# A decoder layer on one core: TensorE's instructions kept in the program's order, and norm sums, rows, cross scores and transposes at other places

## The chip, the core and the metric

The kernel runs on one core of a Trainium2 chip. The metric is the device time of one execution, in microseconds (us). Of the core's engines the text speaks of TensorE (PE, matmuls; PEld are its weight loads), VectorE (DVE), ScalarE (ACT), GpSimd (POOL) and SyncE (SP), whose queue issues most of the DMAs.

## The reference

One layer on x of 256 tokens by 1024, in fp32, with RMSNorm ahead of each part:

```
x = x + 1/2 * SwiGLU_1(RMSNorm(x))
h = RMSNorm(x); q, k, v = split(h @ w_in)     # 12 heads dilated attention, 4 heads block attention, head width 64
x = x + concat(RMSNorm(group A), RMSNorm(group B)) @ w_out
x = x + CrossAttn(RMSNorm(x), RMSNorm(mem))   # 4 heads of width 256, 256 memory tokens
x = x + 1/2 * SwiGLU_2(RMSNorm(x))
out = RMSNorm(x)
rms_norm(x, g) = x * rsqrt(mean(x * x) + 1e-6) * g
```

With 256 tokens there is one block, and the patterns together come down to causal attention with a table per head and distance (the bias, plus the log of how many patterns reach a distance).

## The kernel before

Activations lie transposed, features on the partitions and the 256 tokens in the free dimension. Each fp32 weight tile (128 x 1024, 512 KB) is loaded by SP's queue into one of 4 `raw` buffers and split into one of 8 `w` buffers: a high part (ACT, L122) and the rest, the low part (DVE, L123). Activations are split in the same way into slots (`split`, L310 and L311, or L313 and L314 where a gain is applied). A product is the sum of high x high, high x low and low x high: `mmT_run` does the first two in one 512 wide pass (L221, the slot holds high and low side by side) and the third in a 256 wide pass (L225); `mm3` (L185 to L187) does three passes, `mm2` (L202, L203) is used for the cross output. PSUM is a pool of 8 banks.

The stages in order, by the trace: start and first chunk of gate_up1 (0 to 36 us), gate_up1 (to 139), downT (to 201), `qkv` and `attend` for two head groups (to some 283), cross keys and values (to 340), w_out (to 363), `cross_qp` with the cross scores (to 397), `cross_o` and w_co (to 424), gate_up2 (to 550), the second down product and the tail.

A norm (`Stats`) is deferred: the products run on x times gain without the factor 1/rms, which is applied to their result. `add` sums squares (ACT L327, GpSimd L332). `_col` sums over the partitions with two matmuls by ones (L344), scales (`ms`, DVE L347), takes the power -1/2 on GpSimd (`col`, L349) and writes it on two diagonals (`dg`, L353). `_rows` spreads it over all partitions with two matmuls (L359) and copies the result to `R` (L361).

Where such side work stands is set by a clock in the program: each matmul helper calls `tick` with a duration, `later(delay, fn)` puts `fn` on a list, and `fn` is written out once the clock has passed. `done` (L335) places `_col` at `delay` and `_rows` at `delay + gap`; `scores` and `turn` of `cross_qp` are placed in the same way (L623 and L648), as are `bias_table` (L88, its matmul L95) and the eight gathers from its scratch table. `cross_qp`'s `scores(h)` takes 12 passes for two token blocks, a softmax on DVE and ACT (`cmx`, `cnm`, `cpt`, `crl`, L634 to L644); `turn(h)` transposes the result (L652).

What is so written is then ordered once more by the scheduler of the tile framework, engine by engine. Only `start()` stands under `tc.manual_schedule()` and keeps the written order:

```
    with tc.manual_schedule():
        pu0 = start()
    hid = gate_up(w_gu1, xs, st, (None, bias_table), (pg0, pu0))
```

In `qkv` each 256 wide block of q and k is put together from its two halves and scaled by R at once (`scaled`, L284). In `start` the gain row `grow` is loaded on ACT's queue behind the first quarter of x.

Of the kernel before, what the change touches and what calls it, by code (L numbers as in the profile page):

```python
# [16 lines left out]
P = 128  # L17
# [11 lines left out]
def layer_kernel(ctx, tc, x_in, mem_in, g_ffn1, w_gu1, w_dn1, g_mix, w_in, rel_bias, g_out_a, g_out_b,  # L29
# [13 lines left out]
    def bank():  # L43
        return psp.tile([P, 512], F32, tag="bank", name="bank")
# [43 lines left out]
    def bias_table():  # L88
# [4 lines left out]
        nc.sync.dma_start(rbt, rel_bias)  # L93
        ps = bank()
# [221 lines left out]
    class Stats:  # L316
# [18 lines left out]
        def done(self, rows=True, delay=7.0, gap=4.5):  # L335
            later(delay, self._col)
            if rows:
                later(delay + gap, self._rows)
            return self
# [118 lines left out]
    def qkv(g, xs, st):  # L458
        q, k, v = slot(F32), slot(F32), slot(F32)
        for j, base_a, base_b in ((0, 0, 2304), (1, 768, 2560), (2, 1536, 2816)):  # L460
            wk = colchunk(w_in, base_a, 512) if g == 0 else colchunk2(w_in, base_a + 512, base_b)
            if j == 2:
                for tb in range(2):
                    ps = bank()
                    proj(ps, wk, xs, tb)
                    nc.scalar.activation(v[:, tb * 512:tb * 512 + 512], ps, AF.Copy, scale=st.column(tb))
                continue
            for blk, ps in enumerate(projT(wk, xs, 4, spread=(g == 0 and j == 0))):
                dst = (q, k)[j][:, blk * 256:(blk + 1) * 256]
                scaled(dst, [ps], st.rows(), (0.125, 1.0)[j])  # L470
        return q, k, v
# [149 lines left out]
    def cross_qp(xs, K, st):  # L621
# [3 lines left out]
        def scores(h):  # L625
# [20 lines left out]
            later(3.8, turn, h)  # L646
# [12 lines left out]
        for c in range(2):  # L659
            for blk, ps in enumerate(projT(colchunk(w_cq, c * 512, 512), xs, 4, spread=(c == 0))):  # L660
# [7 lines left out]
                if blk % 2:  # L668
                    later(1.8 + (2.0 * (blk // 2) if c == 0 else 0.0), scores, c * 2 + blk // 2)
# [29 lines left out]
    def start():  # L699
        load_x(0, 256)  # L700
        nc.scalar.dma_start(grow[0:8], g_ffn1.rearrange("l (k p) -> (l k) p", p=P))
# [40 lines left out]
        for k in range(KT):  # L742
# [4 lines left out]
            if k == 5:  # L747
                up.extend(colchunk(w_gu1, FF, 512))
                keep(3)
                st.done(delay=7.5)  # L750
# [14 lines left out]
    hid = gate_up(w_gu1, xs, st, (None, bias_table), (pg0, pu0))  # L765
    xs, st, block = next_x("mix")
    downT(w_dn1, hid, block)
    st.done()

    OT = [slot(F32), slot(F32)]  # L770
    stA, stB = Stats(768), Stats(256)
    ot = []

    def head_pair(kt, op):
        st = stA if kt < 6 else stB
        st.add(op)
        if kt == 5:
            st.done(delay=5.0)
            later(11.0, lambda: out_split(OT, stA.rows(), range(3), ot))
        elif kt == 7:  # L780
            st.done(delay=5.0)
            later(11.0, lambda: out_split(OT, stB.rows(), range(3, 4), ot))

    mxs, mst = mem_side()
    qkv0 = qkv(0, xs, st)
    attend(0, *qkv0, OT, 7.0, head_pair)
    qkv1 = qkv(1, xs, st)
    attend(1, *qkv1, OT, 6.0, head_pair)
    K = cross_k(mxs, mst)
    cross_v(mxs, mst, 0)  # L790
    cross_v(mxs, mst, 1)
    until(lambda: len(ot) == 4)
    xs, st, block = next_x("cross")
    addT(w_out, ot, block)
    st.done(rows=False)
    PT = cross_qp(xs, K, st)
    OT = []
    cross_o(V, PT, OT, (0, 1))
    xs, st, block = next_x("ffn2")
    addT(w_co, OT, block, 4, lambda: cross_o(V, PT, OT, (2, 3)))  # L800
    st.done()

    xt = []

    def to_tokens():
        xt2 = const.tile([P, 2, D], F32, tag="big", name="xt", bufs=2)
        for tb in range(2):
            t = xt2[:, tb]
            for hf in range(2):
                ps = bank()  # L810
                for i in range(4):
                    nc.tensor.transpose(ps[:, i * P:(i + 1) * P], X[hf * 4 + i][:, tb * P:(tb + 1) * P], ident)
                nc.vector.tensor_copy(t[:, hf * 512:hf * 512 + 512], ps)
            xt.append(t)

    hid = gate_up(w_gu2, xs, st, (None, to_tokens))
    gfin = const.tile([P, D], F32, tag="big", name="gfin", bufs=2)
    nc.scalar.dma_start(gfin, g_final.unsqueeze(0).broadcast_to([P, D]))
    HALVES = ((0, 512), (512, 512))
    ps = [[bank() for _ in HALVES] for _ in range(2)]  # L820

    def step(k, tb, w, p, c0, n, first, last):
        h, l = act(hid, k)
        t = slice(tb * P, tb * P + P)
        mm3(p, h[:, t], l[:, t], w[:, 0, c0:c0 + n], w[:, 1, c0:c0 + n], k == first, k == last)

    TAIL = 4
    rest = []
    for k in range(FK):
        w = wload((lambda raw: raw, w_dn2[0, k * P:(k + 1) * P, :], 1024))  # L830
        if k < FK - TAIL:
            for tb in range(2):
                for i, (c0, n) in enumerate(HALVES):
                    step(k, tb, w, ps[tb][i], c0, n, 0, FK - TAIL - 1 if (tb, i) == (1, 1) else FK - 1)
        else:
            rest.append((k, w))

    def add_down(tb, p, c0, n):
        nc.vector.scalar_tensor_tensor(xt[tb][:, c0:c0 + n], p, 0.5, xt[tb][:, c0:c0 + n], OP.mult, OP.add)

    add_down(1, ps[1][1], 512, 512)
    late = [bank()[:, :256] for _ in range(2)]
    PIECES = (((0, 512, ps[0][0], 0), (512, 512, ps[0][1], 0)),
              ((0, 512, ps[1][0], 0), (512, 256, late[0], FK - TAIL), (768, 256, late[1], FK - TAIL)))
    for tb in range(2):
        ss = small.tile([P, 3], F32, tag="fss", name="fss")
        ms = small.tile([P, 3], F32, tag="fms", name="fms")
        junk = work.tile([P, 1024], BF, tag="u1", name="junk")
        xg = slot(F32)
        for i, (c0, n, p, first) in enumerate(PIECES[tb]):  # L850
            sl = slice(c0, c0 + n)
            for k, w in rest:
                step(k, tb, w, p, c0, n, first, FK - 1)
            add_down(tb, p, c0, n)
            nc.scalar.activation(junk[:, sl], xt[tb][:, sl], AF.Square, accum_out=ss[:, i:i + 1])
            nc.vector.tensor_scalar(ms[:, i:i + 1], ss[:, i:i + 1], 1.0 / D, ms[:, i - 1:i] if i else 1e-6,
                                    OP.mult, OP.add)
            nc.vector.tensor_tensor(xg[:, sl], xt[tb][:, sl], gfin[:, sl], OP.mult)
        r = small.tile([P, 1], F32, tag="fr", name="fr")
        nc.gpsimd.tensor_tensor(r, ms[:, len(PIECES[tb]) - 1:len(PIECES[tb])], mhalf[:, 0:1], OP.pow)  # L860
        o = out[0, tb * P:(tb + 1) * P]
        nc.vector.tensor_scalar(xg[:, 0:512], xg[:, 0:512], r, None, OP.mult)
        nc.sync.dma_start(o[:, 0:512], xg[:, 0:512])
        nc.scalar.activation(xg[:, 512:1024], xg[:, 512:1024], AF.Copy, scale=r)
        nc.scalar.dma_start(o[:, 512:1024], xg[:, 512:1024])
# [44 lines left out]
```

## Time and profile before

| | us |
|---|---|
| median of 3 runs | 618.31 |
| lowest, highest | 616.53, 618.38 |
| the profiled execution | 619.02 |
| its span, first to last instruction | 617.1 |
| TensorE busy in it | 601.6 (97%) |
| VectorE busy | 446.0 (72%) |
| ScalarE busy | 350.3 (57%) |
| GpSimd busy | 57.5 (9%) |
| mean granted TensorE clock | 0.997 |

Busy time is the time in which an engine has an instruction under way. A row of a timeline has the start in us, the duration of the run of like instructions in us, the engine, the line, the operation, what is written and read, and how many; a bracket at its end gives the idle time of the engine just before it and what ended that. Matmuls overlap, so the starts tell their pace better than their durations.

### The profile page before, as it was taken

The page shows a single profiled execution, that of the slowest core. Times are in us where ns is not written, and L with a number is a line of the kernel's source. Part 1 is how long each engine was busy: PE and PEld are TensorE (multiplying, and loading weights), DVE is VectorE, ACT ScalarE, POOL GpSimd, SP SyncE. Part 2 cuts the span into 40 slices and gives each one's busy share as a digit, 9 for nine tenths or more (in the row PEclk, how much of TensorE's full clock was granted, in tenths as well). Part 3 has the DMA queues.
Part 4 walks back from the last instruction along what each step waited for, and adds up shares of the span by engine and source line. Part 5 has one row for each costly group of instructions (what it writes and reads, how often), then busy time and mean ns, then how long its engine had stood idle before and what let it go on. Part 6 is the DMA issues. An engine that isn't in the chain of part 4 may idle for free.

```text
span 617.1 us, 9493 instructions
## 1 busy us (share of the span) xinstructions
PE 601.6 (97%) x3488; PEld 518.0 (84%) x3488; DVE 446.0 (72%) x764; ACT 350.3 (57%) x614; POOL 57.5 (9%) x90
## 2 busy tenths in 40 slices
PE   7999999999999899999999999999999999999995
PEld 7987888888899788877877888888888888888885
DVE  3888648898574767775888788868888788794424
ACT  5757426665463666554756566757564565664313
POOL 0000300000010231121311031003100000000000
PEclk9999999999999999999999999999999999999998
DMA  7776996677856637335344646334656646576501
GB/s 233 248 224 195 228 230 203 204 229 229 246 186 198 191 121 237 104 124 185 104 137 141 211 160 206 102 104 138 204 162 213 205 159 223 165 244 202 166 1 68
DMA packets 58989, 110.02 MB, mean 178 GB/s; under 512 B 3760, under 2 KB 14608, under 8 KB 58944
## 3 DMA queue, kind: packets, MB, share of 16 engines
q1 hardware_dynamic: 56848, 104.44, 53.9%
q0 software_dynamic: 832, 2.88, 2.7%
q10 hardware_dynamic: 1264, 2.10, 0.9%
q8 instruction: 27, 0.44, 0.3%
q14 instruction: 18, 0.15, 0.1%
HBM read 107.58 MB, written 1.84 MB: 177 GB/s over the span
## 4 chain that ended last, share of the span: by engine, by line
PE 84%; DVE 6%; ACT 3%; DMA 3%; issue 2%; POOL 1%; ACTq 0%; POOLq 0%
PE bank L221 39%; PE bank L225 20%; PE bank L186 6%; PE bank L185 6%; PE bank L187 6%; DVE w L123 3%; ACT w L122 2%; DMA raw<-in_w_ffn_gu_dram 1%; PE bank L235 1%; PE bank L484 1%; PE bank L531 1%; PE bank L515 1%; DMA raw<-in_w_co_dram 1%; DVE slot L314 1%; DMA grow<-in_g_ffn_dram 1%
## 5 line engine op out<-in xcount | busy, mean ns | idle before, releaser
L221 PE MATMUL bank<-slot,w 128*128 128x512 f32 x1162 | 364.6, 397 | 1.3 <-DVE g L282 0.8
L123 DVE TENSOR_TENSOR w<-raw,w 128x1024 fp32r<-128x1024 f32 (+1 forms) x197 | 239.0, 1227 | 72.9 <-ACT w L122 72.1
L122 ACT ACTIVATE w<-raw 128x1024 fp32r<-128x1024 f32 (+1 forms) x197 | 201.8, 1050 | 96.4 <-PE bank L187 41.2
L225 PEld LDWEIGHTS bank<-slot,w 128*128 128x128 f32 x1162 | 213.8, 188 | 49.1 <-issue 1.5
L225 PE MATMUL bank<-slot,w 128*128 128x256 f32 x1162 | 227.2, 280 | 0.0
L221 PEld LDWEIGHTS bank<-slot,w 128*128 128x128 f32 x1162 | 179.9, 189 | 6.3 <-issue 1.7
L267 ACT ACTIVATE hv<-bank 128x256 f32<-128x256 f32 x120 | 44.0, 376 | 32.6 <-PE bank L225 27.1
L185 PE MATMUL bank<-w,slot 128*128 128x512 f32 (+1 forms) x156 | 60.7, 389 | 0.0
L186 PE MATMUL bank<-w,slot 128*128 128x512 f32 (+1 forms) x156 | 60.1, 385 | 0.0
L187 PE MATMUL bank<-w,slot 128*128 128x512 f32 (+1 forms) x156 | 59.9, 384 | 0.0
L185 PEld LDWEIGHTS bank<-w,slot 128*128 128x128 f32 x156 | 29.3, 188 | 6.1 <-issue 0.5
L187 PEld LDWEIGHTS bank<-w,slot 128*128 128x128 f32 x156 | 29.3, 188 | 5.9
L310 ACT ACTIVATE slot<-u 128x512 fp32r<-128x512 f32 x22 | 13.9, 630 | 35.7 <-DVE u L405 35.7
L186 PEld LDWEIGHTS bank<-w,slot 128*128 128x128 f32 x156 | 29.4, 188 | 5.4
L332 POOL TENSOR_TENSOR ssq<-ssq,sq 128x256 f32<-128x256 f32 x28 | 24.2, 865 | 71.6 <-ACT sq L327 71.1
L268 DVE TENSOR_TENSOR u<-bank,hv 128x256 f32<-128x256 f32 x40 | 16.8, 421 | 10.8 <-ACT hv L267 10.7
L314 DVE SCALAR_TENSOR_TENSOR slot<-X,gT,slot 128x256 fp32r<-128x256 f32 x30 | 19.9, 673 | 6.4 <-ACT slot L313 6.3
L400 ACT ACTIVATE g<-g 128x512 f32<-128x512 f32 x22 | 13.8, 631 | 18.7 <-DVE g L282 18.7
L268 DVE TENSOR_TENSOR g<-bank,hv 128x256 f32<-128x256 f32 x40 | 16.4, 421 | 10.6 <-ACT hv L267 10.6
L502 ACT ACTIVATE pt<-pt,nm 128x128 f32<-128x128 f32 (+1 forms) x32 | 14.2, 445 | 15.1 <-DVE nm L500 15.1
L332 POOL TENSOR_TENSOR ssq<-sq 128x256 f32<-128x256 f32 x6 | 5.2, 870 | 182.1 <-ACT sq L327 182.1
L313 ACT ACTIVATE slot<-X,gT 128x256 fp32r<-128x256 f32 x30 | 14.9, 506 | 12.3 <-DVE X L293 12.3
(132 smaller groups left out, 523.4 us busy)
## 6 DMA issues: line engine op xcount, KB each, us to landing
raw<-in_w_ffn_gu_dram SPq DMA_DIRECT2D x88, 512.0 KB, 4.7
raw<-in_w_ffn_down_dram SPq DMA_DIRECT2D x44, 512.0 KB, 4.6
raw<-in_w_ckv_dram SPq DMA_DIRECT2D x16, 512.0 KB, 6.0
raw<-in_w_in_dram SPq DMA_DIRECT2D x12, 512.0 KB, 3.7
raw<-in_w_in_dram SPq DMA_DIRECT2D x24, 256.0 KB, 4.1
raw<-in_w_out_dram SPq DMA_DIRECT2D x8, 512.0 KB, 5.1
raw<-in_w_cq_dram SPq DMA_DIRECT2D x8, 512.0 KB, 6.0
raw<-in_w_co_dram SPq DMA_DIRECT2D x8, 512.0 KB, 4.0
```

The source lines that it names most:

```text
L122: nc.scalar.activation(w[:, 0, a:b], raw[:, a:b], AF.Copy)
L123: nc.vector.tensor_tensor(w[:, 1, a:b], raw[:, a:b], w[:, 0, a:b].bitcast(F32), OP.subtract)
L185: nc.tensor.matmul(ps, ah, bh, start=start, stop=False)
L186: nc.tensor.matmul(ps, al, bh, start=False, stop=False)
L187: nc.tensor.matmul(ps, ah, bl, start=False, stop=stop)
L221: nc.tensor.matmul(ps, w[:, 0, o + blk * P:o + (blk + 1) * P], both(xs, k), start=k == first, stop=False)
L225: nc.tensor.matmul(ps[:, :256], w[:, 1, o + blk * P:o + (blk + 1) * P], both(xs, k)[:, :256], start=False, stop=k == last)
L267: nc.scalar.activation(t, ps[:, 256:], AF.Copy)
L268: nc.vector.tensor_tensor(out, ps[:, :256], t, OP.add)
L313: nc.scalar.activation(h, src, AF.Copy, scale=g)
L314: nc.vector.scalar_tensor_tensor(l, src, g, h.bitcast(F32), OP.mult, OP.subtract)
L332: (eng or nc.gpsimd).tensor_tensor(new, self.ss, sq, OP.add)
```

## The change

Everything behind `start()` goes under `tc.manual_schedule(engines={PE})`: TensorE keeps the written order, the other engines are still ordered by the scheduler. The matmul of the bias table and what follows from it become `bias_rows`, placed 4.0 behind the loads. The default delay of a norm's sums goes from 7.0 to 9.5; the first norm's gap from 4.5 to 2.8; the delays of head group B from 5.0 and 11.0 to 8.0 and 14.0. `qkv` only puts the halves of q and k together, and scales q in one instruction and k in two once the key product is done. The cross scores of the first two heads go from 1.8 and 3.8 to 2.6 and 4.6, the transposes from 3.8 to 5.0. The gain row is issued ahead of x.

```diff
@@ bias_table
         nc.sync.dma_start(rbt, rel_bias)
+        later(4.0, bias_rows, lnt, oht)
+
+    def bias_rows(lnt, oht):
         ps = bank()
         nc.tensor.matmul(ps[:16, :NB], rbt, oht, start=True, stop=True)
...
@@ Stats
-        def done(self, rows=True, delay=7.0, gap=4.5):
+        def done(self, rows=True, delay=9.5, gap=4.5):
             later(delay, self._col)
@@ qkv
             for blk, ps in enumerate(projT(wk, xs, 4, spread=(g == 0 and j == 0))):
-                dst = (q, k)[j][:, blk * 256:(blk + 1) * 256]
-                scaled(dst, [ps], st.rows(), (0.125, 1.0)[j])
+                halves((q, k)[j][:, blk * 256:(blk + 1) * 256], ps)
+            if j == 1:
+                for t, scale in ((q, 0.125), (k[:, :512], 1.0), (k[:, 512:], 1.0)):
+                    r = st.rows().unsqueeze(1).broadcast_to([P, t.shape[-1] // 256, 256])
+                    nc.vector.scalar_tensor_tensor(v3(t), v3(t), scale, r, OP.mult, OP.mult)
@@ cross_qp
-            later(3.8, turn, h)
+            later(5.0, turn, h)
...
-                    later(1.8 + (2.0 * (blk // 2) if c == 0 else 0.0), scores, c * 2 + blk // 2)
+                    later(2.6 + 2.0 * (blk // 2) if c == 0 else 1.8, scores, c * 2 + blk // 2)
@@ start
+        nc.scalar.dma_start(grow[0:8], g_ffn1.rearrange("l (k p) -> (l k) p", p=P))
         load_x(0, 256)
-        nc.scalar.dma_start(grow[0:8], g_ffn1.rearrange("l (k p) -> (l k) p", p=P))
...
-                st.done(delay=7.5)
+                st.done(delay=7.5, gap=2.8)
@@ after start()
-    hid = gate_up(w_gu1, xs, st, (None, bias_table), (pg0, pu0))
...
+    with tc.manual_schedule(engines={mybir.EngineType.PE}):
+        hid = gate_up(w_gu1, xs, st, (None, bias_table), (pg0, pu0))
...
@@ head_pair
-            st.done(delay=5.0)
-            later(11.0, lambda: out_split(OT, stB.rows(), range(3, 4), ot))
+                st.done(delay=8.0)
+                later(14.0, lambda: out_split(OT, stB.rows(), range(3, 4), ot))
```

Line numbers of the changed kernel are 3 to 7 higher: L221 and L225 become L224 and L228, L185 to L187 become L188 to L190, L202 and L203 become L205 and L206, L123 becomes L126, L311 becomes L314.

TensorE's order, the first cross head's scores, before. `bank_4011` and its like take the query product (L221, L225; `w_` is a weight tile), `bank_4022` and `bank_4041` the scores of the two token blocks; `slot_3965` is that head's query.

```order
L221 MATMUL bank_4011<-slot_3604,w_3998 128x512 x2
L225 MATMUL bank_4011<-slot_3604,w_3998 128x256 x2
L221 MATMUL bank_4011<-slot_3605,w_4003 128x512 x2
L185 MATMUL bank_4022<-slot_3175,slot_3965 128x256
L185 MATMUL bank_4041<-slot_3175,slot_3965 128x256
L225 MATMUL bank_4011<-slot_3605,w_4003 128x256 x2
L221 MATMUL bank_4011<-slot_3606,w_4008 128x512 x2
L186 MATMUL bank_4022<-slot_3175,slot_3965 128x256
L187 MATMUL bank_4022<-slot_3175,slot_3965 128x256
L186 MATMUL bank_4041<-slot_3175,slot_3965 128x256
L187 MATMUL bank_4041<-slot_3175,slot_3965 128x256
L225 MATMUL bank_4011<-slot_3606,w_4008 128x256 x2
```

The same place in the changed kernel, where `bank_4003` takes the query product, `bank_4019` and `bank_4038` the scores and `slot_3957` is the query.

```order
L224 MATMUL bank_4003<-slot_3598,w_4000 128x512 x2
L228 MATMUL bank_4003<-slot_3598,w_4000 128x256
L188 MATMUL bank_4019<-slot_3167,slot_3957 128x256
L189 MATMUL bank_4019<-slot_3167,slot_3957 128x256
L190 MATMUL bank_4019<-slot_3167,slot_3957 128x256
L188 MATMUL bank_4019<-slot_3167,slot_3957 128x256
L189 MATMUL bank_4019<-slot_3167,slot_3957 128x256
L190 MATMUL bank_4019<-slot_3167,slot_3957 128x256
L188 MATMUL bank_4038<-slot_3167,slot_3957 128x256
L189 MATMUL bank_4038<-slot_3167,slot_3957 128x256
L190 MATMUL bank_4038<-slot_3167,slot_3957 128x256
```

The passes of a head now stand in one run behind the last L224 of the block, where matmuls of the query product had stood between them.

VectorE's order ahead of that head's query split, before (`ms` to `dg` are the norm's steps, `hq` is the sum of the halves of a query block, the low parts of weight tiles are the L123).

```order
L123 TENSOR_TENSOR w_4319<-raw_4317,w_4319 128x1024
L347 TENSOR_SCALAR ms_3933<-bank_3930 128x2
L123 TENSOR_TENSOR w_4324<-raw_4322,w_4324 128x1024
L353 TENSOR_SCALAR dg_3937<-ident_83,col_3935 128x128
L353 TENSOR_SCALAR dg_3939<-ident_83,col_3935 128x128
L634 TENSOR_SCALAR c16_4029<-col_3935 128x1
L634 TENSOR_SCALAR c16_4048<-col_3935 128x1
L634 TENSOR_SCALAR c16_4071<-col_3935 128x1
L634 TENSOR_SCALAR c16_4090<-col_3935 128x1
L123 TENSOR_TENSOR w_4329<-raw_4327,w_4329 128x1024
L268 TENSOR_TENSOR hq_3966<-bank_3886,hv_3967 128x256
L123 TENSOR_TENSOR w_4334<-raw_4332,w_4334 128x1024
```

The same stretch in the changed kernel.

```order
L126 TENSOR_TENSOR w_4316<-raw_4314,w_4316 128x1024
L126 TENSOR_TENSOR w_4321<-raw_4319,w_4321 128x1024
L350 TENSOR_SCALAR ms_3939<-bank_3936 128x2
L356 TENSOR_SCALAR dg_3943<-ident_83,col_3941 128x128
L356 TENSOR_SCALAR dg_3945<-ident_83,col_3941 128x128
L271 TENSOR_TENSOR hq_3958<-bank_3878,hv_3959 128x256
L640 TENSOR_SCALAR c16_4026<-col_3941 128x1
L640 TENSOR_SCALAR c16_4045<-col_3941 128x1
L640 TENSOR_SCALAR c16_4069<-col_3941 128x1
L640 TENSOR_SCALAR c16_4088<-col_3941 128x1
L126 TENSOR_TENSOR w_4326<-raw_4324,w_4326 128x1024
L314 TENSOR_TENSOR slot_3957<-hq_3958,slot_3957 128x256
```

`ms` stood behind the split of w_co's first tile (`w_4319`) and now stands behind that of its third (`w_4321`, which was `w_4329`); `hq` stays between the third and the fourth, and now has the norm's steps right ahead of it.

TensorE's order at the end of the cross output of heads 2 and 3, before. `bank_4410` and `bank_4418` take head 3's output, `bank_4519` and `bank_4536` the second half of the columns of w_co, `bank_4337` the first; the slots are the outputs of the heads, `slot_4406` head 2's.

```order
L202 MATMUL bank_4418<-slot_4370,slot_3572 128x512
L203 MATMUL bank_4418<-slot_4370,slot_3572 128x256
L202 MATMUL bank_4418<-slot_4370,slot_3600 128x512
L203 MATMUL bank_4418<-slot_4370,slot_3600 128x256
L221 MATMUL bank_4519<-slot_4214,w_4501 128x512 x2
L225 MATMUL bank_4519<-slot_4214,w_4501 128x256 x2
L221 MATMUL bank_4519<-slot_4310,w_4506 128x512 x2
L225 MATMUL bank_4519<-slot_4310,w_4506 128x256 x2
L221 MATMUL bank_4536<-slot_4214,w_4501 128x512 x2
L221 MATMUL bank_4337<-slot_4406,w_4329 128x512 x2
L225 MATMUL bank_4337<-slot_4406,w_4329 128x256 x2
```

The same place in the changed kernel, where `slot_4398` is head 2's output and `bank_4329` takes the first columns of w_co.

```order
L205 MATMUL bank_4410<-slot_4368,slot_3553 128x512
L206 MATMUL bank_4410<-slot_4368,slot_3553 128x256
L205 MATMUL bank_4410<-slot_4368,slot_3592 128x512
L206 MATMUL bank_4410<-slot_4368,slot_3592 128x256
L224 MATMUL bank_4329<-slot_4398,w_4321 128x512 x2
L228 MATMUL bank_4329<-slot_4398,w_4321 128x256 x2
L224 MATMUL bank_4329<-slot_4418,w_4326 128x512 x2
L228 MATMUL bank_4329<-slot_4418,w_4326 128x256 x2
```

The matmuls into the second half's banks no longer stand between the last L206 and the first product that reads head 2's output.

## Rows read from the trace of the kernel before

**Rows 1.** The page: the span, the busy time of the engines with its share and the count of instructions, and TensorE's granted clock in 40 slices of the span, in tenths of full speed (9 is 90% or more).

```profile
span 617.1 us, 9493 instructions
PE 601.6 (97%) x3488; PEld 518.0 (84%) x3488; DVE 446.0 (72%) x764; ACT 350.3 (57%) x614; POOL 57.5 (9%) x90
PEclk9999999999999999999999999999999999999998
```

**Rows 2.** The waits of TensorE: line and what it waited for, us in total, times, longest.

```profile
PE bank L344 <- POOL ssq L332: 2.7, 3, 1.6
PE bank L221 <- DVE g L282: 0.8, 1, 0.8
```

**Rows 3.** Timeline of TensorE at the start: the gain row's transpose, the first x transposes, the first matmuls.

```profile
5.98 0.27 PE L714 MATMUL bank<-ident,grow 8*128 8x8 f32 x1 [2.13 <-DMA grow<-in_g_ffn_dram]
6.18 1.11 PE L722 MATMUL bank<-ident,slot 128*128 128x128 f32 x4
...
7.95 2.93 PE L235 MATMUL bank<-slot,w 128*128 128x256 f32 x12
```

**Rows 4.** Timelines of TensorE and of VectorE at the end of the first chunk of gate_up1.

```profile
35.98 0.70 PE L221 MATMUL bank<-slot,w 128*128 128x512 f32 x2 [0.24 <-DVE R L361]
...
39.76 0.73 PE L221 MATMUL bank<-slot,w 128*128 128x512 f32 x2 [0.75 <-DVE g L282]
...
38.15 1.22 DVE L123 TENSOR_TENSOR w<-raw,w 128x1024 fp32r<-128x1024 f32 x1 [2.31 <-ACT w L122]
39.29 1.41 DVE L282 TENSOR_TENSOR g<-bank,R 128x256 f32<-128x256 f32 x4
```

**Rows 5.** TensorE at the bias table's matmul and at 97 us, and from the table of windows the stretch 75 to 100 us (from:to, length, then PE, PEld, DVE, ACT and POOL busy with their instructions, the granted clock, the DMA share, GB/s).

```profile
60.29 0.80 PE L95 MATMUL bank<-oht,rbt 32*16 32x383 f32 x2 [0.53 <-DVE w L123]
...
96.43 0.63 PE L221 MATMUL bank<-slot,w 128*128 128x512 f32 x2
97.08 0.50 PE L225 MATMUL bank<-slot,w 128*128 128x256 f32 x2
...
75.00:100.00 25.00, 24.97 (x143) 21.42 (x143) 14.71 (x21) 8.75 (x14) 2.07 (x4) 1.00 0.95 234
```

**Rows 6.** The norm sums of mix on TensorE, what VectorE does beside them, and from the groups by line the scaling of q and k (count, busy us, mean ns, idle before).

```profile
208.62 0.40 PE L225 MATMUL bank<-slot,w 128*128 128x256 f32 x2
210.58 0.61 PE L344 MATMUL bank<-ones,ssq 128*128 128x2 f32 x4 [1.56 <-POOL ssq L332]
...
209.00 0.95 DVE L314 SCALAR_TENSOR_TENSOR slot<-X,gT,slot 128x256 fp32r<-128x256 f32 x1
...
L284 DVE SCALAR_TENSOR_TENSOR slot<-slot,R 128x256 f32<-128x256 f32 x16 | 6.3, 426 | 0.0
```

**Rows 7.** The cross norm and the first cross scores: TensorE, VectorE and GpSimd; the last row is GpSimd's `col` of the mix norm, at 211 us.

```profile
376.01 0.63 PE L221 MATMUL bank<-slot,w 128*128 128x512 f32 x2
377.11 0.51 PE L185 MATMUL bank<-slot 128*128 128x256 f32 x2 [0.47 <-ACT slot L310]
...
382.37 0.64 PE L221 MATMUL bank<-slot,w 128*128 128x512 f32 x2
...
371.43 0.15 DVE L347 TENSOR_SCALAR ms<-bank 128x2 f32<-128x2 f32 x1
...
374.78 1.23 DVE L123 TENSOR_TENSOR w<-raw,w 128x1024 fp32r<-128x1024 f32 x1 [0.75 <-ACT w L122]
...
371.65 1.61 POOL L349 TENSOR_TENSOR col<-ms,mhalf 128x2 f32<-128x2 f32 x1 [3.84 <-DVE ms L347]
...
211.46 0.72 POOL L349 TENSOR_TENSOR col<-ms,mhalf 128x2 f32<-128x2 f32 x1 [0.94 <-DVE ms L347]
```

**Rows 8.** The first product of w_co: TensorE, then VectorE.

```profile
396.85 0.70 PE L221 MATMUL bank<-slot,w 128*128 128x512 f32 x2
...
400.90 0.30 PE L652 MATMUL bank<-ident,cpt 128*128 128x128 f32 x1 [0.55 <-DVE crl L643]
401.47 0.73 PE L221 MATMUL bank<-slot,w 128*128 128x512 f32 x2 [0.27 <-DVE slot L311]
...
399.29 1.21 DVE L123 TENSOR_TENSOR w<-raw,w 128x1024 fp32r<-128x1024 f32 x1
400.41 0.35 DVE L644 TENSOR_SCALAR cpt<-cpt,crl 128x256 f32<-128x256 f32 x1
...
400.74 0.68 DVE L311 TENSOR_TENSOR slot<-on,slot 128x512 fp32r<-128x512 f32 x1
```

**Rows 9.** The end of the cross output of heads 2 and 3: TensorE, then VectorE.

```profile
407.60 0.73 PE L221 MATMUL bank<-slot,w 128*128 128x512 f32 x2
...
408.40 0.63 PE L221 MATMUL bank<-slot,w 128*128 128x512 f32 x2
...
409.10 1.09 PE L221 MATMUL bank<-slot,w 128*128 128x512 f32 x4
...
405.99 1.23 DVE L123 TENSOR_TENSOR w<-raw,w 128x1024 fp32r<-128x1024 f32 x1 [1.97 <-ACT w L122]
...
408.61 1.33 DVE L311 TENSOR_TENSOR slot<-on,slot 128x512 fp32r<-128x512 f32 x2
```

More of the change, by code (lines that the diff above doesn't have):

```diff
@@ L764, in layer_kernel @@
         pu0 = start()
-    hid = gate_up(w_gu1, xs, st, (None, bias_table), (pg0, pu0))
[L766 to L777, printed above, removed]
-            st.done(delay=5.0)
-            later(11.0, lambda: out_split(OT, stA.rows(), range(3), ot))
-        elif kt == 7:
-            st.done(delay=5.0)
-            later(11.0, lambda: out_split(OT, stB.rows(), range(3, 4), ot))
@@ L784, in layer_kernel @@
[L784 to L806, printed above, removed]
-        for tb in range(2):
[L808 to L865, printed above, removed]
```

87 lines of the change are left out of this document (added).

## The prediction

> **What bounds the kernel now.** I read the busy shares first, then the list of TensorE's waits, then the timeline of TensorE around each wait, and last the timelines of the engines named there. The first view says that TensorE is busy 601.6 of 617.1 us and that its granted clock is at full level in every slice but the last [rows 1]. So there is no second bound to lift: the change can only take waits out of TensorE's queue or put some in. The second view says that the norm sums (L344) waited three times for the squares' sum on GpSimd, 2.7 us together, and the first SwiGLU chunk once for VectorE's L282, 0.8 us [rows 2]. The remaining waits are single rows, shown where they are used. A wait costs a little more than the idle time in its row: between the L225 pair that starts at 208.62 and the L344 at 210.58 lie 1.96 us, 0.23 of them for the pair itself, so 1.73 where the row says 1.56 [rows 6]. I add 0.17 us to each idle time for that.
>
> **The change part by part.** A plus is time won, a minus time lost, all against the profiled execution (619.02 us).
>
> *Start.* The gain row is now issued ahead of x on ACT's queue. Before, L714 waited 2.13 us for it at 5.98, and the x transposes followed at 6.18 [rows 3]. The x they need is now issued one DMA issue later, so it lands about when the transposes began before. 0 (bounds -0.3 and +0.3).
>
> *Rows of the first norm, gap 4.5 to 2.8.* The two matmuls go 15 places forward. Before, L221 waited 0.24 us for the row copy at 35.98 and 0.75 us at 39.76 for L282, because VectorE, which works in order, split a weight tile from 38.15 to 39.37 first [rows 4]. With the copy some 2 us earlier the first L282 stands ahead of that split, and both waits go: 0.24 + 0.75 + 2 x 0.17 = **+1.3** (bounds 0.4 and 1.35).
>
> *Bias table.* L95 goes 24 places later, some 4.2 us; it waited 0.53 us at 60.29 [rows 5]. **+0.55** (0 to 0.7). Its DMA burst (75 to 100 us, DMA share 0.95) then starts later by about 3.5 us against TensorE's work, while the weights ahead of it are further along; the short wait inside the burst, a gap of 0.2 to 0.3 us at 97.08 [rows 5], should go: **+0.3** (this is where the slower rival sits).
>
> *Norm sums, delay 7.0 to 9.5.* For mix, L344 goes 14 places later, 2.45 us, more than its wait of 1.73. But the matmuls that now stand ahead of it need the last normalised half, which VectorE finishes at 209.00 + 0.95 [rows 6]; some 0.85 us of wait stays in another place. **+0.9** (0.5 to 1.7). The two other waits of L344 (2.7 - 1.56 = 1.14 us [rows 2, 6], with 0.17 each 1.45) are those of group B and of ffn2; their sums go 11 and 14 places later, 2 us or more. **+1.4** (0.7 to 1.45).
>
> *Query scaled once.* 16 instructions of 0.43 us [rows 6] become six, which by width I price at up to one weight split each (1.23 us [rows 7]): 6 x 1.23 = 7.4 against 6.8 at most. VectorE does them while TensorE runs the value product, and the first attention scores are many us behind. 0; were the cover gone, one instruction, 1.2 us.
>
> *First two cross heads.* The scheduler had put L221 between the score passes. From 376.01 to 382.37 lie 6 L221, 6 L225 and 24 score passes; at 0.232 us for a 512 wide and 0.118 for a 256 wide pass (the estimates that fit undisturbed stretches: two of each take 0.70 from 408.40 to 409.10 [rows 9]) that is 4.93 us, so 1.4 us were waits [rows 7]. Now the 12 passes of a head stand in one run. On VectorE the norm's `ms` moves behind the split of w_co's third tile, which ended at 376.0 where `ms` had run at 371.43 [rows 7]. The chain is ms, col on GpSimd, two dg, the half sum, the split into high and low with one more weight split between: the high part some 0.9 us late, the low 1.2, the second half 0.55 and 0.3, about 3.0 us. **-1.6** (-0.5 to -2.5). For col I take 0.72 us, the row where VectorE had nothing to do but wait for it, and not the 1.61 us beside a weight split [rows 7]; with 1.61 the loss is 0.9 more. *A rule stands beside these two rows: the Trainium skill, "SBUF — State Buffer" (on the shared port pair), says that VectorE and GpSimd lock one pair of ports for a whole instruction and the loser is blocked. By that rule col is short whenever VectorE's next instruction waits for it, as it would here, and the loss stays 1.6; the two rows agree, 0.72 and 1.61.* For the fourth head's last quarter of q I take a third of a weight split, **-0.35** (0 to -1.2).
>
> *First product of w_co.* The transposes at delay 5.0 came between the matmuls of the first slot; there TensorE waited 0.55 and 0.27 us, 1.16 together [rows 8]. Now the 16 matmuls of the first slot run through, four take 0.70, so from 396.85 to 399.65, and then the second slot's low part is wanted. It was ready at 401.4, behind a weight split from 399.29 and one scaling; now it has two scalings of 0.35 ahead of it, so 401.8 to 402.0 [rows 8]. The wait is some 2.35 us: **-1.2** (0 to -2).
>
> *Cross output of heads 2 and 3.* At 407.60 the scheduler had drawn matmuls of w_co's second half forward; they covered the split that ends the third slot, 408.61 and on [rows 9]. In stated order that slot is asked for at 407.60, and its low part ends near 409.3, since VectorE first ends the weight split begun at 405.99: a wait of **-1.85** (-1.2 to -2.2).
>
> Sum: 1.3 + 0.55 + 0.3 + 0.9 + 1.4 = 4.45 won, 1.6 + 0.35 + 1.2 + 1.85 = 5.0 lost; net 0.55 slower, 619.6 for the profiled execution. That one stands 0.7 above the median of the three runs, 618.31, so I forecast **618.9 us**.
>
> **Rivals.** *Faster.* The gains rest on waits that rows show; the losses on an order that no run has had. If the scores and w_co products come as late as their inputs (two of the four losses not there, 3.05 us), it is 615.8; with none, 613.9. For it: each lost wait is under 2.5 us, as long as some ten matmuls. Against it: VectorE's row at cross q, where `ms` stands behind two more splits.
>
> *Slower, the bias burst.* The transfers L95 sets free collide with the weights of the next chunks. Before, one weight split was just in time (the gap at 97.08), at DMA share 0.95 [rows 5]. If the burst moves 3.5 us back against the same weights, which gained at most 1.9 us by then, the tiles come 2.5 to 4 us late in all, and 618.9 becomes 621.4 to 622.9. It decides from the point where a tile's lead before the burst is under 2 us. *Slower, the cross stage.* All four losses at their bounds, 2.9 us more, halved since they share the queue: about 620.4.
>
> *The clock.* The granted clock stayed at full level through a wait of 1.56 us [rows 1, 6]. The new waits are longer, up to 2.4 us, and three come within 35 us. If the clock fell at each, and a stretch such as the first 12 L235 (2.93 us [rows 3], where 12 of 0.118 need 1.4) ran slowly, four would cost 6 us: 625. *The Trainium skill, "TensorE: Matmul & The Clock Gate" (HAM oscillation), says that TensorE's idle spells between groups of matmuls can bring the clock down again; the trace shows it only after the last matmul.*
>
> **How the numbers follow.** The forecast, gains and losses near balance, 617 to 620.4: 0.45. Faster rival: 0.25. Bias burst: 0.14. Cross stage worse: 0.12. Clock: 0.04. What a measurement can tell from no change is 0.3%, 1.9 us: faster is under 616.4, slower over 620.2. Faster takes most of its rival and a little of the forecast's edge, 0.26; slower takes the burst, the clock, most of the worse cross stage and the edge, 0.30; 0.44 is left. The range of 8 in 10 leaves out a tenth on each side: 615.2 to 622.0.
>
> **What would show it.** In the profile after: no wait of L221 before 40 us; L95 without one; L347 (L344 before) waiting once, for under 1 us in all. New rows: L188 or L189 waiting for the split of q near 374, L224 waiting near 396 and near 404 for the split L314, each 1 to 2.5 us. If the waits near 374 to 404 sum to under 2 us, the faster rival holds; if L224 waits for a weight's split (L126) between 80 and 110 us, the burst does. The forecast is wrong if TensorE's idle time falls by over 2 us or grows by over 2.

## The result, and the profile after

Six executions of each kernel: before 616.89 us in the median (three more than the table had, and lower), the changed kernel 621.05. The ratio is 1.0062, with a 95% interval of 1.0039 to 1.0084: slower by 0.6%. The medians lie 4.2 us apart. The forecast was 618.9 within 615.2 to 622.0; the time lies inside the range, on the slower side, and the likeliest case (no measurable change) was not what came. The profiled execution took 621.25 us, that of before 619.02.

The page of the changed kernel, to be set beside [rows 1].

```profile
span 619.5 us, 9485 instructions
...
PEclk9999999999999999999999998999999999999999
```

TensorE's granted clock has a dent in one slice, at 372 to 387 us, which the trace of before does not have. The waits of TensorE, as in [rows 2]:

```profile
PE bank L224 <- DVE slot L314: 3.6, 2, 1.9
PE bank L728 <- DMA slot<-in_x_dram: 3.2, 1, 3.2
...
PE bank L189 <- DVE slot L314: 0.9, 1, 0.9
PE bank L224 <- DVE slot L317: 0.8, 1, 0.8
PE bank L188 <- ACT slot L313: 0.6, 2, 0.4
PE bank L566 <- DMA slot<-in_mem_dram: 0.4, 1, 0.4
```

The waits for L282, for the norm sums and for the bias table are gone; L224 waits twice for a slot's split, L188 and L189 for the query's. To see what each is worth I set the start of the same matmul in both traces side by side. A step is what the difference changed by from the row above; plus is time lost.

| up to | after minus before, us | step | forecast |
|---|---|---|---|
| the first chunk's last matmuls (34.7 us) | +0.79 | +0.79 | 0 |
| past the first SwiGLU product (51 us) | -0.71 | -1.50 | -1.3 |
| past the bias table (66 us) | -1.30 | -0.59 | -0.55 |
| past its DMA burst (122 us) | -1.60 | -0.30 | -0.3 |
| past the norm of mix and mem's transposes (224 us) | -1.80 | -0.20 | -0.9 |
| past group B's norm (336 us) | -2.68 | -0.88 | -1.4, with ffn2's |
| first cross output (391 us) | +0.09 | +2.77 | +1.6 |
| its third head (405 us) | +1.39 | +1.30 | +0.35 + 1.2 |
| the third slot of w_co (408 us) | +3.14 | +1.75 | +1.85 |
| past ffn2's norm, and to the end | +2.34 | -0.80 | (above) |

Three steps are off: the start, the mix norm, and the first cross scores. The timeline of TensorE at these scores, answering to [rows 7]:

```profile
374.52 0.28 PE L228 MATMUL bank<-slot,w 128*128 128x256 f32 x1
375.15 0.39 PE L188 MATMUL bank<-slot 128*128 128x256 f32 x1 [0.36 <-ACT slot L313]
376.41 0.39 PE L189 MATMUL bank<-slot 128*128 128x256 f32 x1 [0.88 <-DVE slot L314]
376.64 0.28 PE L190 MATMUL bank<-slot 128*128 128x256 f32 x1
377.20 0.38 PE L188 MATMUL bank<-slot 128*128 128x256 f32 x1 [0.28 <-ACT slot L313]
377.65 0.45 PE L189 MATMUL bank<-slot 128*128 128x256 f32 x1
377.91 0.42 PE L190 MATMUL bank<-slot 128*128 128x256 f32 x1
378.12 0.42 PE L188 MATMUL bank<-slot 128*128 128x256 f32 x1
...
381.11 0.34 PE L190 MATMUL bank<-slot 128*128 128x256 f32 x1
381.29 0.27 PE L188 MATMUL bank<-slot 128*128 128x256 f32 x1
381.41 0.28 PE L189 MATMUL bank<-slot 128*128 128x256 f32 x1
```

Up to 377.65 these are waits, start to start 0.51, 1.14, 0.44 and 0.33 us more than the passes need. From there to 381.1 nothing waits, and yet the passes start 0.21 us apart, not 0.12. The table of windows over the same stretch (columns as in [rows 5]) says why:

```profile
375.00:378.00 3.00, 1.62 (x6) 1.02 (x7) 2.77 (x6) 1.81 (x6) 0.00 (x0) 0.97 0.92 314
378.00:381.00 3.00, 3.00 (x14) 2.81 (x14) 2.04 (x8) 1.29 (x4) 0.00 (x0) 0.50 0.31 117
381.00:384.00 3.00, 3.00 (x22) 2.82 (x22) 2.06 (x13) 1.82 (x7) 0.00 (x0) 0.96 0.02 5
```

The granted clock fell to 0.50, from 2.4 to 1.2 GHz, when TensorE had been busy 1.62 of 3 us, and was back at 381. From 377.65 to 381.29 lie 13 passes of 256 and two of 512 columns, 2.0 us of work at full clock; they took 3.64, so the fall cost 1.6 us. VectorE's side of the waits, with GpSimd's `col`:

```profile
371.73 1.23 DVE L126 TENSOR_TENSOR w<-raw,w 128x1024 fp32r<-128x1024 f32 x1 [1.74 <-ACT w L125]
372.87 0.15 DVE L350 TENSOR_SCALAR ms<-bank 128x2 f32<-128x2 f32 x1
...
374.23 0.42 DVE L271 TENSOR_TENSOR hq<-bank,hv 128x256 f32<-128x256 f32 x1
...
374.81 1.21 DVE L126 TENSOR_TENSOR w<-raw,w 128x1024 fp32r<-128x1024 f32 x1
375.94 0.42 DVE L314 TENSOR_TENSOR slot<-hq,slot 128x256 fp32r<-128x256 f32 x1
...
373.10 0.70 POOL L352 TENSOR_TENSOR col<-ms,mhalf 128x2 f32<-128x2 f32 x1 [7.93 <-DVE ms L350]
```

`ms` runs right behind the third tile's split, `col` takes 0.70 us, and the low part of the query ends at 376.36 behind the fourth tile's. That is the chain that was forecast. *The Trainium skill, "SBUF — State Buffer" (SBUF: two separate sides), says that the first of a GpSimd instruction and a VectorE instruction with two SBUF inputs holds the shared port pair to its end and blocks the other. Here VectorE only waits for `col`, and its 0.70 us agree.* The two waits of L224:

```profile
402.31 0.50 PE L224 MATMUL bank<-slot,w 128*128 128x512 f32 x1 [1.92 <-DVE slot L314]
...
410.75 0.50 PE L224 MATMUL bank<-slot,w 128*128 128x512 f32 x1 [1.72 <-DVE slot L314]
```

### The profile page after: what moved, and what is told of

It is laid out like the page before. It is cut to its first block, busy times and chain, and to the rows that moved or that the text cites. A ratio compares the mean times of both kernels' runs of the same rounds, so it can differ in the third digit from the quotient of the medians.

```text
span 619.5 us, 9485 instructions
## 1 busy us (share of the span) xinstructions
PE 601.9 (97%) x3488; PEld 519.4 (84%) x3488; DVE 445.0 (72%) x754; ACT 350.7 (57%) x614; POOL 57.0 (9%) x90
## 4 chain that ended last, share of the span: by engine, by line
PE 90%; DVE 4%; DMA 2%; ACT 2%; issue 1%; POOL 0%; ACTq 0%; POOLq 0%; SPq 0%
PE bank L224 41%; PE bank L228 20%; PE bank L188 7%; PE bank L189 7%; PE bank L190 7%; PE bank L238 3%; DVE w L126 2%; PE bank L490 1%; PE bank L537 1%; DMA slot<-in_x_dram 1%; PE bank L521 1%; DVE slot L317 1%; DMA slot<-in_mem_dram 1%; ACT w L125 1%; DMA raw<-in_w_co_dram 1%
## 5 line engine op out<-in xcount | busy, mean ns | idle before, releaser
L224 PE MATMUL bank<-slot,w 128*128 128x512 f32 x1162 | 364.4, 397 | 4.6 <-DVE slot L314 3.6
L126 DVE TENSOR_TENSOR w<-raw,w 128x1024 fp32r<-128x1024 f32 (+1 forms) x197 | 237.5, 1222 | 72.9 <-ACT w L125 72.3
L228 PEld LDWEIGHTS bank<-slot,w 128*128 128x128 f32 x1162 | 214.6, 188 | 49.2 <-issue 1.5
L228 PE MATMUL bank<-slot,w 128*128 128x256 f32 x1162 | 228.2, 280 | 0.0
L224 PEld LDWEIGHTS bank<-slot,w 128*128 128x128 f32 x1162 | 180.0, 189 | 9.3 <-DVE slot L314 4.2
L188 PE MATMUL bank<-w,slot 128*128 128x512 f32 (+1 forms) x156 | 60.8, 390 | 0.0
L189 PE MATMUL bank<-w,slot 128*128 128x512 f32 (+1 forms) x156 | 60.0, 384 | 0.0
L190 PE MATMUL bank<-w,slot 128*128 128x512 f32 (+1 forms) x156 | 59.9, 384 | 0.0
L188 PEld LDWEIGHTS bank<-w,slot 128*128 128x128 f32 x156 | 29.3, 188 | 6.0 <-issue 0.5
L190 PEld LDWEIGHTS bank<-w,slot 128*128 128x128 f32 x156 | 29.3, 188 | 5.9
L189 PEld LDWEIGHTS bank<-w,slot 128*128 128x128 f32 x156 | 29.3, 188 | 5.5
```

Of the source, the lines that this page charges most:

```text
L126: nc.vector.tensor_tensor(w[:, 1, a:b], raw[:, a:b], w[:, 0, a:b].bitcast(F32), OP.subtract)
L188: nc.tensor.matmul(ps, ah, bh, start=start, stop=False)
L189: nc.tensor.matmul(ps, al, bh, start=False, stop=False)
L190: nc.tensor.matmul(ps, ah, bl, start=False, stop=stop)
L224: nc.tensor.matmul(ps, w[:, 0, o + blk * P:o + (blk + 1) * P], both(xs, k), start=k == first, stop=False)
L228: nc.tensor.matmul(ps[:, :256], w[:, 1, o + blk * P:o + (blk + 1) * P], both(xs, k)[:, :256], start=False, stop=k == last)
```

## The experiments

My theory after this: the moved places won what the trace shows; TensorE's stated order lost the two waits of L224 outright; the late `ms` holds the first scores; the waits there let the clock fall, 1.6 us more; and the start lost 0.8 us. Rivals: the later places of scores and transposes lose, not the order; the clock falls at some time whatever TensorE does; the start is absorbed. All ratios are to the kernel before, run beside each experiment.

**The start (e1).**

```diff
-        nc.scalar.dma_start(grow[0:8], g_ffn1.rearrange("l (k p) -> (l k) p", p=P))
         load_x(0, 256)
+        nc.scalar.dma_start(grow[0:8], g_ffn1.rearrange("l (k p) -> (l k) p", p=P))
```

> The changed kernel with x's first quarter issued ahead of the gain row again. Theory start: issued 0.65 us later on ACT's queue, x lands 1.1 us later, and 0.8 us of that is still there at 60 us; so this kernel starts the x transposes near 6.2 us instead of 7.28 and is 0.8 us (0.1%) faster than the changed kernel, a ratio to before of about 1.005. Rival: the start is absorbed by a later wait (weights, the bias burst), ratio unchanged at 1.006.

620.37 us, ratio 1.0053 (1.0037 to 1.0068). By time alone it can't be told from 1.0062; the trace tells it. In the changed kernel, then in this one:

```profile
7.28 1.12 PE L728 MATMUL bank<-ident,slot 128*128 128x128 f32 x4 [3.23 <-DMA slot<-in_x_dram]
```

```profile
5.80 0.27 PE L720 MATMUL bank<-ident,grow 8*128 8x8 f32 x1 [1.95 <-DMA grow<-in_g_ffn_dram]
6.00 1.11 PE L728 MATMUL bank<-ident,slot 128*128 128x128 f32 x4
```

The transposes start 1.3 us earlier, and at the same matmul at 204 us the trace is 1.2 us ahead. In five other kernels with the gain row first they started at 7.41 to 7.66; in four more with x first at 5.79 to 6.01. The later start is the order of the two issues, and up to 204 us nothing absorbs it.

**The order taken back, the places kept (e2).**

```diff
-    with tc.manual_schedule(engines={mybir.EngineType.PE}):
+    if True:
         hid = gate_up(w_gu1, xs, st, (None, bias_table), (pg0, pu0))
```

> The changed kernel with TensorE ordered by the scheduler again everywhere behind the start; all delays, the bias rows and the scaling as changed. Theory order: the stated order costs in the cross stage (the two waits of L224 for the third and second slot, 2.1 and 1.9 us, and part of the 2.9 us at the first scores, 1.7 of them by the lower clock), and the moved places give the gains; so about 5 us faster than the changed kernel, 616, ratio 0.998 to 1.000. Rival delays: the later places of scores and transposes cost, not the order; then 620 to 621, ratio 1.005.

616.96 us, ratio 1.0000 (0.9987 to 1.0013): 4 us better than the changed kernel, though not better than before. The rival falls: the kernel with the later places and without the stated order loses nothing. The third slot of w_co is covered again, as L224 at 407.00 shows, 0.24 us behind the last L206:

```profile
376.45 0.39 PE L188 MATMUL bank<-slot 128*128 128x256 f32 x1 [0.78 <-ACT slot L313]
377.71 0.38 PE L189 MATMUL bank<-slot 128*128 128x256 f32 x1 [0.87 <-DVE slot L314]
...
406.76 0.27 PE L206 MATMUL bank<-slot 128*128 128x256 f32 x1
407.00 0.73 PE L224 MATMUL bank<-slot,w 128*128 128x512 f32 x2
```

But the waits at the first scores are nearly as long as in the stated order, so these are not the order's: they come from the late `ms`. What the scheduler does there is to put the second token block's first passes ahead of those that need the second half of the query, which then do not wait, and in this execution the clock did not fall.

**The order alone (e5).** The kernel before, with everything behind `start()` under `tc.manual_schedule(engines={PE})`.

> The kernel before with TensorE kept in the stated order and nothing else changed. Theory order: all of the loss in the cross stage is the order's, all of the gain before 340 us is the moved places'; so the early waits stay (L221 at 36 and 40 us, L95, L344), and the waits at the first scores and at the second and third slot of w_co come on top, 4 to 6 us: 621 to 623, ratio 1.007 to 1.010, with the clock at 0.50 for some 3.5 us behind one of those waits. Rival: the later places are part of the loss; then the stated order alone loses less, 618 to 620, ratio 1.002 to 1.005.

626.05 us, ratio 1.0147 (1.0119 to 1.0176): slower than either theory gave. The stated order also puts the norm sums nearer to their inputs than the scheduler had: L344 waited 2.49 and 1.54 us where it had waited 1.56 and 0.64, and the clock fell right behind the first of these waits.

```profile
209.52 0.89 PE L344 MATMUL bank<-ones,ssq 128*128 128x2 f32 x4 [2.49 <-POOL ssq L332]
...
328.96 0.61 PE L344 MATMUL bank<-ones,ssq 128*128 128x2 f32 x4 [1.54 <-POOL ssq L332]
```

```profile
206.00:210.00 4.00, 1.51 (x10) 1.14 (x9) 2.85 (x5) 1.61 (x4) 1.51 (x2) 0.96 0.81 227
210.00:212.00 2.00, 2.00 (x7) 1.71 (x8) 0.64 (x3) 0.00 (x0) 0.73 (x1) 0.50 0.76 243
```

So the delays that the change moves are there for the stated order: without them it loses 9 us in the median, and 6 in its two executions with a mean clock of 0.995; with them 4. The other four executions have a mean clock of 0.987 to 0.990, and took 626 to 629 us; I have no trace of those.

**The cross norm earlier (e3).**

```diff
-        st.done(rows=False)
+        st.done(rows=False, delay=7.0)
```

> The changed kernel with the cross norm's sums at delay 7.0 as before, so that VectorE's ms stands two weight splits earlier. Theory norm: the late ms holds the query's split; waits at the first scores fall from 2.4 to 1.6 us and, if the clock stays up, another 1.7 us goes: 0.8 to 2.5 us faster than the changed kernel, ratio 1.002 to 1.005. Rival: the run of 12 passes waits for the query's split whatever the norm does; ratio 1.006.

620.09 us, ratio 1.0051 (1.0033 to 1.0068): just above the expected range, and by time alone not to be told from the changed kernel's 1.0062. In the trace the step at the first scores is gone almost whole: it is 3.31 us ahead of before at the first score and 3.26 at the first cross output, where the changed kernel went from 1.96 ahead to 0.09 behind. But the fall of the clock came later, behind the wait for the second slot of w_co:

```profile
396.00:400.00 4.00, 2.08 (x14) 1.67 (x13) 3.98 (x9) 2.10 (x5) 0.00 (x0) 1.00 0.25 43
400.00:403.00 3.00, 3.00 (x13) 2.60 (x12) 0.83 (x3) 1.13 (x2) 0.00 (x0) 0.51 0.88 259
```

**The waits filled (e4, e6).** First those of the first score block alone (e4), then those of L224 too (e6). `zero` is a tile of zeros, so the sums stay what they are.

```diff
+                        busy(sp, kh, (4, 3)[et], et == 0)
                         nc.tensor.matmul(sp[:, :256], qh[:, t], kh, start=False, stop=False)
+                        busy(sp, kh, (9, 3)[et], False)
...
+        def busy(sp, kh, n, first):
+            for i in range(n):
+                nc.tensor.matmul(sp[:, :256], zero, kh, start=first and i == 0, stop=False)
```

> The changed kernel with 19 matmuls by a tile of zeros, 256 wide, put into the waits of the first score block (4, 9, 3 and 3 of them, 2.2 us at full clock); the sums are unchanged. Theory clock: in the changed kernel the granted clock fell to half for 3.5 us behind these waits, which doubled what ran there, 1.7 us; with TensorE busy the clock stays at 1.00, the waits are filled and not lengthened by more than 0.3 us, so 1.4 us faster where the clock had fallen, ratio 1.003 to 1.004. Rival: the fall has to do with the time in the kernel or the DMA load, not with the waits; then the clock row still shows 0.50 near 378 us and the time is equal or 0.3 us longer, ratio 1.006 to 1.007.

622.14 us, ratio 1.0077 (1.0063 to 1.0091). Neither theory's number: the clock held at 1.00 from 372 to 382 us, and fell at the next wait instead.

```profile
372.00:382.00 10.00, 9.59 (x68) 8.74 (x67) 7.42 (x24) 5.62 (x14) 0.70 (x1) 1.00 0.72 228
396.00:402.00 6.00, 3.85 (x21) 2.96 (x20) 5.75 (x21) 4.20 (x12) 0.00 (x0) 1.00 0.31 96
402.00:404.00 2.00, 2.00 (x9) 1.83 (x10) 1.21 (x2) 0.60 (x1) 0.00 (x0) 0.60 0.83 250
```

Then, as well, in `addT` ahead of the second and the third slot's first product:

```diff
+                        if (k, blk) == (2, 0):
+                            idle(b[0], 17, both(src, 0))
...
+                        if (k, blk) == (early, 0):
+                            idle(b[0], 15, both(src, 0))
```

> The kernel with zeros in the first score block's waits, with 17 and 15 more such matmuls ahead of the second and the third slot's first product of w_co, which fill the 2.1 and 1.9 us waited there; the sums are unchanged. Theory clock: every wait of over 1 us in the cross stage is filled, so no fall of the clock is left; as the fill of the first block alone only moved the fall to the next wait, this kernel is 1.7 us faster than that one: 620.4, ratio 1.005, granted clock 1.00 in every stretch from 14 to 600 us. Rival: the fall comes at some time in any case, by the chip's load; then a stretch at 0.50 is found elsewhere and the ratio stays at 1.008.

620.40 us, ratio 1.0049 (1.0036 to 1.0061): 1.7 us faster than the one above, as expected, by 32 matmuls more that compute nothing. Against the changed kernel (1.0062) the fillers win nothing that is clear of noise. The granted clock over the whole middle, and the fillers where the waits had been:

```profile
14.00:600.00 586.00, 583.97 (x3429) 504.73 (x3428) 432.94 (x728) 339.23 (x590) 55.23 (x82) 1.00 0.58 180
```

```profile
399.31 2.16 PE L442 MATMUL bank<-slot,zero 128*128 128x256 f32 x17
401.38 0.50 PE L225 MATMUL bank<-slot,w 128*128 128x512 f32 x1
```

All its executions had a mean clock of 0.998 or 0.999; of the changed kernel's six, four had 0.994 or 0.995 and took 620.8 to 622.3 us, two had 0.998 and took 619.4 and 619.9. So the fall comes from the waits: fill one, and it moves to the next; fill all, and it is gone.

**The scheduler for the cross stage only, and x first (e7).**

```diff
+    if True:
         PT = cross_qp(xs, K, st)
...
+    with tc.manual_schedule(engines={mybir.EngineType.PE}):
         hid = gate_up(w_gu2, xs, st, (None, to_tokens))
```

> The changed kernel with the stated order ending ahead of the cross queries and beginning again at the second SwiGLU, the scheduler ordering TensorE between them, and x's first quarter issued first. Theory: it keeps the gains up to 340 us (2.7 us), gives the start back (0.8 to 1.1) and loses only the waits at the first scores (some 1.9 us) and none to the clock: the trace ends about 3 us ahead of the kernel before; 614, ratio 0.995 to 0.997. Rival: the scheduler's places are bound to its order of the whole program, and the cross stage alone comes out as in the changed kernel; 620, ratio 1.005.

614.71 us, ratio 0.9958 (0.9944 to 0.9972): as expected, 6 us under the changed kernel and faster than before.

**The same, and mem's second half later (e8).**

```diff
-            later(4.0, turn, hf, m)
+            later((4.0, 5.5)[hf], turn, hf, m)
```

> The kernel that leaves the cross stage to the scheduler and issues x first, with the transposes of mem's second half placed 1.5 us later (delay 5.5 instead of 4.0 behind the load's issue). Theory: the changed kernel's TensorE, 2.4 us ahead at that place, waited 0.4 to 0.9 us for mem's transfer, which had stood hidden before; the wait goes, 0.6 us faster, ratio 0.001 under its sister. Rival: the transposes come later, and the norm sums behind them are waited for instead; no difference.

615.48 us, ratio 0.9969 (0.9956 to 0.9981): not faster. The wait for mem (0.5 us) is gone, and the trace is 0.8 us further ahead at 336 us; the first score begins at 373.12, against 373.07 without the edit. ScalarE's split of w_co's third tile, behind which `ms` stands, in the sister and then here:

```profile
368.56 1.06 ACT L125 ACTIVATE w<-raw 128x1024 fp32r<-128x1024 f32 x1 [1.76 <-PE bank L347]
```

```profile
368.60 1.06 ACT L125 ACTIVATE w<-raw 128x1024 fp32r<-128x1024 f32 x1 [2.84 <-DMA raw<-in_w_co_dram]
```

It waited for the tile's transfer and began no earlier, so the 0.8 us won turned into a longer wait of L188 (1.04 us instead of 0.19), and the clock fell behind it.

**The same as e7, and `ms` out from behind that tile (e10)**, by `delay=7.0` for the cross norm.

> The version in which the cross stage is left to the scheduler and x is issued first, with the cross norm's sums at 7.0 as before. Theory: at the first scores it waited 0.36 and 1.14 us because ms stands behind the split of w_co's third tile; with ms two splits earlier about 0.8 us of that goes: 613.9, ratio 0.9945. Rival: the query's split is held by the next weight split in either order, and the time is the same, 614.7, ratio 0.996.

613.60 us, ratio 0.9934 (0.9919 to 0.9949): the best version, 0.7% under the kernel before, though its interval still touches that of e7. `ms` now runs at 366.60, ahead of both, and L188 does not wait:

```profile
366.60 0.14 DVE L350 TENSOR_SCALAR ms<-bank 128x2 f32<-128x2 f32 x1
```

```profile
372.46 0.28 PE L188 MATMUL bank<-slot 128*128 128x256 f32 x1
373.32 0.39 PE L189 MATMUL bank<-slot 128*128 128x256 f32 x1 [0.57 <-DVE slot L314]
```

**The scaling block by block again (e9).** The changed kernel with `scaled(dst, [ps], st.rows(), ...)` as before.

> The changed kernel with q and k scaled block by block again, 16 instructions of 256 columns. There the first block asks for the norm's rows as soon as the first product is done, so the two row matmuls and the transposes of mem's first half stand in one place about 2 us earlier on TensorE. Theory cover: the scaling's own time is hidden on VectorE in both; what changes is only the place, and mem's second transfer is asked for earlier, so its wait of 0.4 to 1.0 us grows by up to 1 us: 0 to 1 us slower than the changed kernel, ratio 1.006 to 1.008. Rival: the change of instructions on VectorE is itself a gain, some 1.5 us of VectorE's time that a later wait shows; 1.5 us slower or more, ratio above 1.008.

621.52 us, ratio 1.0051 (1.0031 to 1.0070), against 1.0062: no difference. The cover holds. What I had not seen when I predicted is its place: scaling a block asks for the norm's rows, and that brings the row matmuls forward (213.08 us, where the changed kernel has them at 214.60). The longer wait for mem that I expected from this did not come.

## Why the prediction was right in range and short in size

**Right, by the rows.** The waits that the moved places take away: 1.50 for 1.3, 0.59 for 0.55, 0.30 for 0.3, 1.68 for 1.4 (the second and the third only against this one trace of before, as told below). The new waits of the stated order in the cross output: 1.75 for 1.85, and 1.30 for 1.55; the order alone is what they hang on (e2 has neither). The scaling cost nothing. `ms` was late as told, and its waits, 2.4 us by start times, are under the 3.0 forecast.

**Wrong: "the clock".** I gave it 0.04 as a rival and 6 us for four falls. By the mean clock it fell in four of six executions, and in the profiled one it cost 1.6 us. The argument against it, that the clock had stayed up through 1.56 us of wait [rows 6], did not carry: that was one wait, and at the first scores four came within 3 us. *The rule of the Trainium skill that stood beside the rival ("TensorE: Matmul & The Clock Gate", HAM oscillation) has waits between groups of matmuls bring the clock down. Its case is waits for transfers; e4 and e6 show it here of waits for the splits of other engines, and the trace of before did not.* With it, the step at the first scores is 1.1 to 1.2 us of waits more than before and 1.6 of clock. Nor is a fall quite new: of the 45 executions of the kernel before that ran beside the experiments, six have a mean clock of 0.994, and five of these took 618.5 to 619.7 us, where the median of all is 617.2. No trace shows where it fell in them.

**Wrong: the start, 0.** I had x land "about when the transposes began before". It landed 1.1 us later than that (7.28), 0.8 us of which stayed; my bound was 0.3. The 0.8 is against one trace. At the matmul that starts at 28.10 us before, the six traces with the gain row first are 0.20 to 1.28 us behind, the five others with x first 0.34 to 1.49 ahead; so by an estimate from these twelve traces, six and six with that of before among the second, the order of the two issues costs 1.6 us on the average. The spread within each group goes with the moment at which the first passes go over from one start in 0.21 us to one in 0.12: 12.3 us in the trace of before, 9.2 in that of e10, where the twelve passes of [rows 3], 2.93 us before, took less:

```profile
7.76 2.31 PE L238 MATMUL bank<-slot,w 128*128 128x256 f32 x12
```

The clock column has 1.00 on both sides of that moment, so the traces do not say what sets it.

**Wrong: mix, 0.9 forecast, 0.2 measured.** The wait went as told, down to 0.91 us for the normalised half; but mem's second transfer was issued no earlier (215.29 us, 215.13 before), while TensorE came to its transposes before 219.72 us, where it had come to them at 221.30; so it waited where the transfer had been hidden:

```profile
208.42 1.20 PE L224 MATMUL bank<-slot,w 128*128 128x512 f32 x4 [0.75 <-DVE slot L317]
...
219.72 1.06 PE L566 MATMUL bank<-ident,slot 128*128 128x128 f32 x8 [0.42 <-DMA slot<-in_mem_dram]
```

**Wrong: what the sum was set against.** The two profiled executions differ by 2.2 us, the medians by 4.2, since the profiled one of before lies 2.1 above its median. I put a part of its waits on the account of the change. The kernel of e5 has the same program up to 200 us; there L95 did not wait (in [rows 5] it did, 0.53 us), and it is 1.1 us ahead of the trace of before at the same matmul at 110 us:

```profile
59.19 0.40 PE L221 MATMUL bank<-slot,w 128*128 128x512 f32 x1
59.52 0.81 PE L95 MATMUL bank<-oht,rbt 32*16 32x383 f32 x2
```

So about 1 us of the gains that I counted was that execution's own: 0.58 of it lies at the bias table and 0.30 in its DMA burst, the same steps that I had put down to the moved places. The other 1 us fits its start, the slowest of the six with x first: the other five are 0.97 us ahead of it on the average.

**Luck.** My base, the median of three runs, lay 1.4 us above that of six, and this hid as much of the loss, 4.2 where 0.55 was forecast; from the lower base the range would have ended at 620.6, under the time. My own sign of being wrong, TensorE's idle time growing by over 2 us, was just met: by the two profiles it grew from 15.5 to 17.6.

**The rivals.** Faster (losses that do not come): the losses came. The bias burst: no weight split was waited for between 80 and 110 us. The worse cross stage: its waits stayed within the forecast; the clock was what made it worse.

## What to carry to other kernels

An order fixed by hand is only as good as the delays that stand in it: the scheduler had been covering two waits of 2 us with matmuls of a later product, and fixing the order gave them back. Look for each gap that it covers before taking it away, and fix the order only where the delays were made for it (e7, e10). A wait won early is lost again where a transfer was just hidden. And count gains from waits that more than one execution shows.

## What the runs showed of the hardware that was not expected

The granted clock went from 1.00 to 0.50 behind waits of 0.3 to 1.1 us (start to start) that followed each other closely, as well as behind single waits of 2.5 us (e5); a single wait of 1.33 us in e2 (L347 at 209 us) left it at 1.00, and so did the two of 0.78 and 0.87 us there at the first scores. In the changed kernel it fell behind the first of three such places and not behind the two later ones, 2.1 and 1.9 us long; where the first was filled, it fell at the second (e4). Which of two like waits brings it down, and why it fell in four of the six executions only, no run here shows. Products by zeros in the two waits of L224 were worth 1.7 us where the clock had fallen there (e4 to e6), and nothing clear of noise against the kernel without any.
